# Cross-attention reassociated: query weights times memory keys and memory values times output weights formed once (one decoder layer, one core)

## The chip, the cores and the metric

One core of one Trainium2 chip runs the whole program. The metric is device time in microseconds (us) of one execution, median over the runs. The profile is that of one separately profiled execution; a profile's span runs from its first to its last instruction.

## The reference, cut to what matters

One inference step of a one-layer decoder: a prompt of 2048 tokens and 8 single-token samples, model width 1024, all float32. The layer has two windowed attentions side by side, then cross-attention into 256 memory tokens, then a ConvFFN. The change touches the cross-attention alone:

```python
def memory_kv(mem, g_mem, w_mem_kv):
    kv = rms_norm(mem, g_mem) @ w_mem_kv            # 256 memory tokens
    k, v = jnp.split(kv, 2, axis=-1)                # 4 heads of 256 each
    ...
def cross_attention(h, mk, mv, w_xq, w_xo):
    q = (h @ w_xq).reshape(N, T, X_HEADS, X_HEAD_DIM)
    s = jnp.einsum('nthd,nmhd->nhtm', q, mk) * (X_HEAD_DIM ** -0.5)
    p = jax.nn.softmax(s, axis=-1)
    o = jnp.einsum('nhtm,nmhd->nthd', p, mv).reshape(N, T, D_MODEL)
    return o @ w_xo
```

The prompt's memory keys and values are computed and are outputs too. Each of the 8 samples has memory keys and values of its own, from a cache.

## The kernel before, in words

**Stages.** First the combined input projection of the prompt, with the windowed attentions woven between its tiles; then the memory keys and values (`mem_pieces`, L1640) woven between the last attention work and the first merges; then four chunks of 512 tokens. A chunk c is `pre` (L1266: output projection `w_out`, cross-attention) and `ffn` (L1442). The 8 samples ride along as 8 more columns (512 to 519): through `w_out` and the query projection in chunk 2, through the cross-attention's output projection and the ConvFFN in chunk 3. In those steps `pieces` (L843) cuts the 520 columns into 256 and 264.

**Products.** A float32 operand is split into a high part (`hi_of`, L107, ScalarE) and the rest (`lo_of`, L118, VectorE), and each product is three matmuls: high by high, low by high, high by low (L862 to L864). Activations live in panels of 128 rows by 520 columns, two parts each, from one tag of 22 buffers (L789).

**Weights.** `WStream` (L126) loads units of 4 x 128 rows by 256 columns (512 KB) into 3 raw buffers in a fixed order (L203), splits each into one of 4 pairs of buffers, and gives them out in the same order. A unit of a 512-column chunk is used by 24 matmuls.

**Cross-attention of one chunk** (L1291 to L1439). For each head `xq` (L1306) makes queries from two units of `w_xq`, scales them by the row norm broadcast over partitions (`r_bc`, L914: one full float32 matmul) and splits them. `scores` (L1345) multiplies queries (stationary, 128 tokens) by memory keys (256 moving columns) and does the softmax; `transp` (L1375) turns the probabilities; `pvx` (L1389) multiplies by the memory values; `gemm_full` (L873) applies `w_xo` from 8 units. `load_kv` (L1294) fetches and splits keys and values per head in every chunk from DRAM, where `evac_mem` (L1623) has put them.

**Samples.** `qxs` gets the samples' queries from `xq` in chunk 2; `xs_begin` (L1179) turns them and stores them; the other `cross_steps` (L1225) run in pieces during the ConvFFN of chunk 2 and leave the result in `oxs`, which `pvx` copies into the panels in chunk 3.

**Order.** Program order gives the priority; at build the framework places each engine's instructions by that priority and a timeline of its own (L1753), so later work can be pulled into gaps, within dependences and buffers. All loads and stores but a few go through SyncE's one queue. `tick` (L821) issues one side step per weight unit, and every fourth time a copy of 1 MB of the caches.

Of the kernel before, what the change touches and what calls it, by code (L numbers as in the profile page):

```python
# [18 lines left out]
D = 1024  # L19
# [16 lines left out]
def tile_layer(ctx: ExitStack, tc: tile.TileContext, I, C, O):  # L36
# [49 lines left out]
    mk_d = [dram.tile([128, 512], F32, tag=f"mk_d{h}", name=f"mk_d{h}") for h in range(4)]  # L86
    mv_d = dram.tile([256, 1024], F32, tag="mv_d", name="mv_d")
# [38 lines left out]
    class WStream:  # L126
        RAW, SPL = 3, 4

        def __init__(self):
            self.units = []  # L130
            self.raw, self.spl = {}, {}
            self.nr = self.ns = self.pos = 0

        def add(self, w, k0, nk, c0, ncol):
            self.units.append((w, k0, nk, c0, ncol))
# [10 lines left out]
        def split_to(self, i):  # L146
            while self.ns <= min(i, len(self.units) - 1):
# [13 lines left out]
        def get(self):  # L161
            self.split_to(self.pos)
            u = self.spl.pop(self.pos)
            self.pos += 1
            return u

# [58 lines left out]
    cache_steps.append(lambda: dma(out=p_mv, in_=mv_d))  # L225
# [590 lines left out]
    qxs = sbA.tile([128, 8, NS], F32, tag="qxs", name="qxs")  # L816
    oxs = sbA.tile([128, 2, 8, NS], F32R, tag="oxs", name="oxs")
# [361 lines left out]
    def xs_begin():  # L1179
        p = [bankA("t"), bankA("t")]  # L1180
        row = panel32("qxrow")
        for k in range(8):
            nc.tensor.transpose(p[k // 4][:NS, (k % 4) * 128:(k % 4) * 128 + 128], qxs[:, k, :], ident)
        for i in range(2):
            vec.tensor_copy(out=row[:NS, 512 * i:512 * i + 512], in_=p[i][:NS])
        dma(out=qx_d, in_=row[:NS, 0:1024])

# [28 lines left out]
    def xs_fin():  # L1216
# [5 lines left out]
        hi_of(oxs[:, 0], v, "a")  # L1222
        lo_of(oxs[:, 1], v, oxs[:, 0])

    cross_steps = [xs_begin] + [xs_score(n) for n in range(NS)] + \  # L1225
# [40 lines left out]
    def pre(c, oT, begin):  # L1266
# [24 lines left out]
        q_t, kv_t, p_t = {}, {}, {}  # L1291
        R = [None]

        def load_kv(h):  # L1294
            a, b = panel("mk"), panel("mv")
            for pn, src in ((a, mk_d[h]), (b, mv_d[:, 256 * h:256 * h + 256])):
                raw = small("kv")[:, 0:512]
                if pn is a:
                    dma(out=raw, in_=src)
                else:  # L1300
                    dma(out=raw.rearrange("p (k c) -> p k c", k=2), in_=src.rearrange("(k p) c -> p k c", p=128))
                hi_of(pn[:, 0, 0:512], raw, "a")
                lo_of(pn[:, 1, 0:512], raw, pn[:, 0, 0:512])
            kv_t[h] = (a, b)

        def xq(h):  # L1306
            pn = [panel("q"), panel("q")]
            load_kv(h)

            def first():  # L1310
                if h == 1:
                    nrm.r_tok()
                return W.get()

            def second():
                if h == 1:
                    R[0] = nrm.r_bc()
                    for go in late:
                        go()
                return W.get()  # L1320

            def ev(m, pi, a, b, p):
                scaled(m, a, b, p[:, 0:b - a])

            def scaled(m, a, b, p):
                f = small("qf")
                vec.tensor_tensor(out=f[:, a:b], in0=p, in1=R[0][:, a:b], op=ALU.mult)
                if b > 512:
# [5 lines left out]
            def raw(m, pi, a, b, p):  # L1334
                if pi == 0:
                    fs[m] = small("qf")
# [420 lines left out]
```

## Time and profile before

| | |
|---|---|
| median of 3 runs | 3233.0 us (3232.56 to 3245.07) |
| profiled execution, its own time | 3230.24 us |
| its span | 3228.5 us, 58044 instructions |
| TensorE matmuls | 22290, busy 96% of the span |
| VectorE / ScalarE / GpSimd busy | 67% / 44% / 31% |
| mean granted TensorE clock | 0.984 |

The span is 1.7 us shorter than the profiled execution's own time, which is 2.8 us under the median. "Busy" of TensorE counts overlapping matmuls' records as one stretch; how fast it goes is read from the distance between starts. In the chain of waits each piece is what the end waited for at that moment.

### The profile page before, as it was taken

How to read it: one execution, taken by the hardware profiler on the slowest of the kernel's cores; microseconds unless marked ns; L12 is line 12 of the kernel's file. 1: busy time of each engine (PE TensorE's matmuls, PEld its weight loads, DVE VectorE, ACT ScalarE, POOL GpSimd, SP SyncE). 2: the span in 40 equal slices, each digit the busy share in tenths (PEclk: the TensorE clock that was granted, in tenths of full speed). 3: DMA queues.
4: the chain of work that ended last, by engine and by line, in shares of the span. 5: the costliest groups of instructions: out<-in, count | busy, mean ns of one | idle time of the engine just before them, and what ended most of it. 6: DMA issues, size and time to landing. Idle time of an engine off the chain costs nothing.

```text
span 3228.5 us, 58044 instructions
## 1 busy us (share of the span) xinstructions
PE 3100.5 (96%) x22290; PEld 2713.9 (84%) x22290; DVE 2147.1 (67%) x4299; ACT 1417.1 (44%) x2793; POOL 1013.7 (31%) x959
## 2 busy tenths in 40 slices
PE   8999989889888999999999999999999999999999
PEld 8998888788877888888887778798877778999998
DVE  7687677787886667665567766555687665554544
ACT  3555654666665444223444333444433343432322
POOL 2711613224244046342205524320554332110102
PEclk9999999998899999999999999999999999999999
DMA  6899999999897346664525555453476445223231
GB/s 211 249 253 237 270 243 230 252 242 220 191 231 230 119 152 209 204 198 162 207 97 184 169 168 183 144 196 111 159 240 235 157 151 179 73 86 96 89 95 64
DMA packets 621837, 580.14 MB, mean 180 GB/s; under 512 B 264140, under 2 KB 554104, under 8 KB 620432
## 3 DMA queue, kind: packets, MB, share of 16 engines
q1 hardware_dynamic: 616808, 572.21, 60.6%
q10 hardware_dynamic: 4608, 4.20, 0.4%
q8 instruction: 175, 2.87, 0.4%
q14 instruction: 102, 0.84, 0.1%
q0 software_dynamic: 144, 0.03, 0.0%
HBM read 457.55 MB, written 136.66 MB: 184 GB/s over the span
## 4 chain that ended last, share of the span: by engine, by line
PE 64%; DVE 7%; DMA 7%; POOL 3%; issue 3%; ACT 2%; SPq 1%; POOLq 0%; DVEq 0%; ACTq 0%
PE g L863 18%; PE g L862 18%; PE g L864 18%; DMA pT<-p 4%; PE s L1358 1%; PE g L1398 1%; PE o L585 1%; DVE wl L120 1%; DVE p L570 1%; DVE sm L556 1%; DMA kx<-in_cache_mem_k_dram 1%; PE g L672 1%; PE g L674 1%; PE g L673 1%; DMA mrg<-o_d 1%
## 5 line engine op out<-in xcount | busy, mean ns | idle before, releaser
L120 DVE TENSOR_TENSOR wl<-wr,wh 128x1024 fp32r<-128x1024 f32 (+1 forms) x406 | 535.7, 1320 | 359.8 <-ACT wh L110 358.3
L110 ACT ACTIVATE wh<-wr 128x1024 fp32r<-128x1024 f32 (+1 forms) x444 | 460.8, 1040 | 674.5 <-PE g L864 382.7
L863 PE MATMUL g<-h,wl 128*128 128x512 f32 (+2 forms) x2080 | 729.5, 351 | 0.0
L862 PE MATMUL g<-h,wh 128*128 128x512 f32 (+2 forms) x2080 | 729.5, 351 | 0.0
L864 PE MATMUL g<-h,wh 128*128 128x512 f32 (+2 forms) x2080 | 725.1, 349 | 0.0
L862 PEld LDWEIGHTS g<-h,wh 128*128 128x128 f32 x2080 | 390.7, 188 | 58.6 <-issue 1.0
L864 PEld LDWEIGHTS g<-h,wh 128*128 128x128 f32 x2080 | 391.2, 188 | 55.2 <-issue 0.5
L863 PEld LDWEIGHTS g<-h,wl 128*128 128x128 f32 x2080 | 390.8, 188 | 54.9 <-issue 1.4
L672 PE MATMUL g<-wh,xh 128*128 128x256 f32 x1152 | 340.4, 296 | 1.1 <-ACT z L383 0.7
L674 PE MATMUL g<-wh,xl 128*128 128x256 f32 x1152 | 333.1, 289 | 0.3 <-DVE xl L120 0.3
L673 PE MATMUL g<-wl,xh 128*128 128x256 f32 x1152 | 331.8, 288 | 0.0
L862 PE MATMUL g<-act,wh 128*128 128x512 f32 (+2 forms) x880 | 310.4, 353 | 8.2 <-ACT act L110 5.7
L863 PE MATMUL g<-act,wl 128*128 128x512 f32 (+2 forms) x880 | 309.4, 352 | 0.0
L864 PE MATMUL g<-act,wh 128*128 128x512 f32 (+2 forms) x880 | 308.0, 351 | 0.0
L561 ACT ACTIVATE sm<-sm,ost 128x256 f32<-128x256 f32 (+1 forms) x512 | 234.8, 460 | 155.1 <-DVE ost L559 154.4
L892 POOL TENSOR_TENSOR sq<-sq 128x512 f32<-128x512 f32 (+1 forms) x83 | 125.2, 1508 | 484.2 <-ACT sq L887 451.3
L672 PEld LDWEIGHTS g<-wh,xh 128*128 128x128 f32 x1152 | 223.5, 194 | 6.4 <-ACT z L383 0.9
L674 PEld LDWEIGHTS g<-wh,xl 128*128 128x128 f32 x1152 | 222.9, 193 | 4.0 <-DVE xl L120 1.2
L673 PEld LDWEIGHTS g<-wl,xh 128*128 128x128 f32 x1152 | 223.3, 194 | 2.1 <-issue 0.2
L862 PE MATMUL g<-oT,wh 128*128 128x512 f32 (+2 forms) x608 | 216.1, 356 | 4.5 <-ACT oT L110 4.5
L863 PE MATMUL g<-oT,wl 128*128 128x512 f32 (+2 forms) x608 | 215.9, 356 | 0.0
L864 PE MATMUL g<-oT,wh 128*128 128x512 f32 (+2 forms) x608 | 211.6, 355 | 0.0
(353 smaller groups left out, 6084.2 us busy)
## 6 DMA issues: line engine op xcount, KB each, us to landing
wr<-in_w_up_dram SPq DMA_DIRECT2D x176, 512.0 KB
wr<-in_w_down_dram SPq DMA_DIRECT2D x80, 512.0 KB
out_dram<-in_cache_a_k_dram SPq DMA_DIRECT2D x32, 1023.5 KB
out_dram<-in_cache_a_v_dram SPq DMA_DIRECT2D x32, 1023.5 KB
wr<-in_w_in_dram SPq DMA_DIRECT2D x60, 512.0 KB
v<-va_d SPq DMA_DIRECT2D x60, 384.0 KB
wr<-in_w_out_dram SPq DMA_DIRECT2D x32, 512.0 KB
wr<-in_w_xq_dram SPq DMA_DIRECT2D x32, 512.0 KB
```

The lines of the kernel that those rows point to most:

```text
L110: act(out=out, in_=in_, func=ACTF.Copy)
L120: e.tensor_tensor(out=out, in0=in_, in1=hi.bitcast(F32), op=ALU.subtract)
L556: vec.tensor_tensor_reduce(out=sm[:, x, 0:n], in0=S[e][:, u * n:(u + 1) * n], in1=m_, scale=1.0, scalar=-3e38, op0=ALU.add, op1=ALU.max, a ...
L561: act(out=sm[:, x, 0:n], in_=sm[:, x, 0:n], func=ACTF.Exp, scale=0.125, bias=nb[:, x:x + 1], accum_out=job.ost[:, 520 + 4 * i + x:521 + 4 ...
L570: vec.tensor_tensor(out=p2[:, 1], in0=sm[:, :, 0:n], in1=p2[:, 0], op=ALU.subtract)
L672: mm(p[:, 0:256], h[:, kt, :], wh[:, q, :], start=(kt == 0), stop=False)
L673: mm(p[:, 0:256], h[:, kt, :], wl[:, q, :], start=False, stop=False)
L674: mm(p[:, 0:256], l[:, kt, :], wh[:, q, :], start=False, stop=(kt == 7))
L862: mm(o, wh[:, q, c], pn[:, 0, a:b], start=st, stop=False)
L863: mm(o, wl[:, q, c], pn[:, 0, a:b], start=False, stop=False)
L864: mm(o, wh[:, q, c], pn[:, 1, a:b], start=False, stop=en)
L892: pl.tensor_tensor(out=acc[:, 0:self.ncol], in0=acc[:, 0:self.ncol], in1=sq[:, 0:self.ncol], op=ALU.add)
```

## The change

The keys of head h are folded into the query weights (`qk_d` = w_xq_h times keys transposed, 1024 x 256 per head), and the values into the output weights (`vo_d` = values times w_xo_h, 256 x 1024 per head). Both are made once between the attention and chunk 0, stored to DRAM, and streamed as weight units in every chunk. `scores` now multiplies normalised tokens (stationary) by units of `qk_d` (256 moving columns, 1024 deep instead of 256), and the turned probabilities are multiplied by `vo_d` directly; the row norm enters as the scale of the softmax. `xq`, `load_kv`, `pvx` and the query's `r_bc` go. The samples, whose keys are their own, get their query and output projections by themselves from units of `w_xq` (chunk 2) and `w_xo` (chunk 3) that only they use (`sample_rows`). The memory values are turned and stored like the keys, and written to their output from SBUF rather than copied later.

```diff
+        self.whole = set()
...
-            while self.ns <= min(i, len(self.units) - 1):
+            while self.ns <= min(i, len(self.units) - 1) and self.ns not in self.whole:
...
+    def get_whole(self):
+        self.load_to(self.pos)
...
+    for h in range(4):
+        for hf in range(2):
+            W.add(w_xq, 4 * hf, 4, 256 * h, 256, whole=True)
+        for hf in range(2):
+            W.add(w_xo, 2 * h, 2, 512 * hf, 512)
     for c in range(4):
         add_full(w_out)
-        add_full(w_xq)
-        add_full(w_xo)
+        add_full(qk_d)
+        if c == 2:
+            add_full(w_xq)
+        if c == 3:
+            add_full(w_xo)
+        for mps, khs in (((0, 1), (0,)), ((0, 1), (1,)), ((2,), (0, 1)), ((3,), (0, 1))):
+            for kh in khs:
+                for mp in mps:
+                    W.add(vo_d, 4 * kh, 4, 256 * mp, 256)
...
-    cache_steps.append(lambda: dma(out=p_mv, in_=mv_d))
...
-    cross_steps = [xs_begin] + [xs_score(n) for n in range(NS)] + \
+    cross_steps = [xs_score(n) for n in range(NS)] + \
...
         def scores(h):
+            S = [bank("s", 2) if h % 2 == 0 else bank("g", 4) for _ in range(2)]
+            for kh in range(2):
+                w = W.get()
+                for t in range(4):
+                    for q in range(4):
+                        pn = h1[4 * kh + q]
+                        for a, b in ((0, 0), (0, 1), (1, 0)):
+                            mm(S[t // 2][:, t % 2 * 256:t % 2 * 256 + 256], pn[:, a, t * 128:t * 128 + 128], w[b][:, q, :],
...
+                W.ahead(2)
+                tick()
+            if h == 0:
+                r = sbA.tile([128, 4], F32, tag="r16", name="r16", bufs=2)
+                vec.tensor_scalar(out=r, in0=nrm.r_tok()[:, 0:4], scalar1=0.0625, scalar2=None, op0=ALU.mult)
...
+        def sample_rows(scale, done):
+            row = panel32("srow")
+            for mp in range(4):
+                p = bankA("t")
+                for kh in range(2):
+                    wh, wl = W.get()
+                    for q in range(4):
+                        k = 4 * kh + q
+                        parts = [(p[:NS, 0:256], las[:, k, 0:NS], wl), (p[:40, 0:256], las[:, k, :], wh)]
+                        for o, x, w in parts if k else reversed(parts):
+                            mm(o, x, w[:, q, :], start=(k == 0 and w is wh), stop=(k == 7 and w is wh))
+                    W.ahead(2)
...
+        for h in range(4):
+            scores(h)
+            if h:
+                transp(h - 1)
...
+        if s_in:
+            sample_rows(nrm.r[:NS, 4:5], keep_q)
+        if s_out:
+            sample_rows(None, add_xo)
+        gemm_two(pT, ev_xo, lambda: transp(3))
+        gemm_full(pT, pieces(False), ev_xo, range(2, 4))
...
+        dma(out=(p_mk if j < 4 else p_mv)[tok, cols], in_=z)
+        pt = bankA("t")
+        for dt in range(2):
+            nc.tensor.transpose(pt[:, dt * 128:dt * 128 + 128], z[:, dt * 128:dt * 128 + 128], ident)
+        zt = small("mz")[:, 0:256]
+        act(out=zt, in_=pt[:, 0:256], func=ACTF.Copy)
+        dma(out=mkv_d[j].rearrange("p (k t) -> p k t", k=2)[:, :, tok], in_=zt.rearrange("p (k t) -> p k t", k=2))
...
+    def mem_q(h, hf, mk):
+        w = W.get_whole()
+        T = []
+        for dt in range(2):
+            pt = bankA("t")
+            for q in range(4):
+                nc.tensor.transpose(pt[:, q * 128:(q + 1) * 128], w[:, q, dt * 128:dt * 128 + 128], ident)
+            pn = panel("wT")
+            hi_of(pn[:, 0, 0:512], pt, "a")
+            lo_of(pn[:, 1, 0:512], pt, pn[:, 0, 0:512])
+            T.append(pn)
...
+        for fp in range(2):
+            p = bank("g", 4)
+            for f in range(2):
+                fb = 2 * fp + f
+                for dt in range(2):
+                    for a, b in THREE:
+                        mm(p[:, f * 256:f * 256 + 256], T[dt][:, a, fb * 128:fb * 128 + 128],
+                           mk[:, b, dt * 256:dt * 256 + 256], start=(f == 0 and dt == 0 and a + b == 0),
...
+            store_w(p, "a", qk_d[r0:r0 + 256, 256 * h:256 * h + 256].rearrange("(f p) c -> p f c", p=128))
+    def mem_o(h, hf, mv):
+        w = W.get()
+        W.ahead(1)
+        for kb in range(2):
+            p = bank("g", 4)
+            for dt in range(2):
+                for a, b in THREE:
+                    mm(p, mv[:, a, dt * 256 + kb * 128:dt * 256 + kb * 128 + 128], w[b][:, dt, :],
...
+            store_w(p, "v", vo_d[(2 * h + kb) * 128:(2 * h + kb + 1) * 128, 512 * hf:512 * hf + 512])
+    for h in range(4):
+        mk = mem_panel(h)
+        for hf in range(2):
+            mem_q(h, hf, mk)
+        mv = mem_panel(4 + h)
+        for hf in range(2):
+            mem_o(h, hf, mv)
     oT = []
     for go in heads_T(0, oT):
         go()
```

In what is left out, `gemm_two` takes the first four `vo_d` units depth half by depth half, with 24 matmuls of 512 columns each; `mem_panel` loads one `mkv_d` panel (256 KB) and splits it; `store_w` evacuates a bank and stores 256 KB.

## Rows read from the trace of the kernel before

**Rows 1.** The page's first part: busy time (share of the span) and instructions.

```profile
PE 3100.5 (96%) x22290; PEld 2713.9 (84%) x22290; DVE 2147.1 (67%) x4299; ACT 1417.1 (44%) x2793; POOL 1013.7 (31%) x959
```

**Rows 2.** Waits of TensorE, longest in total first: us, times, longest.

```profile
PE o L585 <- DMA pT<-p: 43.1, 34, 2.8
...
PE g L862 <- ACT act L110: 5.7, 2, 4.7
```

**Rows 3.** Busy time by stretch of the span, with granted clock, DMA share, GB/s.

```profile
core 0: us, PE busy (x) PEld busy (x) DVE busy (x) ACT busy (x) POOL busy (x), PEclk, DMA share, GB/s
860.00:980.00 120.00, 100.05 (x1323) 90.24 (x1321) 101.63 (x309) 82.14 (x232) 58.38 (x40) 0.94 1.00 233
980.00:1000.00 20.00, 11.41 (x177) 10.41 (x176) 14.62 (x19) 9.81 (x19) 7.46 (x5) 0.97 1.06 287
1000.00:1040.00 40.00, 40.00 (x181) 32.46 (x180) 24.01 (x38) 17.74 (x29) 12.91 (x10) 0.97 0.65 219
1048.00:1165.00 117.00, 116.42 (x569) 96.64 (x568) 68.71 (x117) 51.77 (x97) 11.35 (x8) 1.00 0.37 124
...
2710.00:2830.00 120.00, 120.00 (x774) 108.77 (x773) 71.19 (x128) 54.34 (x100) 18.02 (x25) 1.00 0.28 90
```

**Rows 4.** The chain of waits in chunk 0's cross-attention: start, us, what.

```profile
1067.40 0.86 PE t L922 x2
...
1107.79 2.78 PE g L1398 x12
1110.57 0.87 PE t L1381 x8
1111.44 2.83 PE s L1358 x24
```

**Rows 5.** TensorE's timeline in chunk 3: start, us, instruction; 6 and 12 starts lie between these.

```profile
2900.01 0.29 PE L862 MATMUL g<-h,wh 128*128 128x264 f32 x1
...
2900.75 0.28 PE L862 MATMUL g<-h,wh 128*128 128x256 f32 x1
...
2902.16 0.28 PE L862 MATMUL g<-h,wh 128*128 128x264 f32 x1
```

**Rows 6.** Line 1358 (scores): weight loads, ns min/median/max, first and last start.

```profile
L1358 PEld LDWEIGHTS s<-mk,q x384: 187/188/192, 1074.6 to 2776.2; 128*128 128x128 f32 x192
```

**Rows 7.** TensorE's timeline, sample columns of the input projection (40 and 8 rows).

```profile
664.48 0.29 PE L771 MATMUL g<-wh,la 128*40 128x256 f32 x1
664.60 0.28 PE L771 MATMUL g<-wl,lb 128*8 128x256 f32 x1
664.72 0.28 PE L771 MATMUL g<-wh,la 128*40 128x256 f32 x1
```

**Rows 8.** Waits of SyncE's queue: us in total, times, longest.

```profile
SPq L141 <- DVE wl L120: 1365.3, 295, 24.7
```

**Rows 9.** ScalarE and VectorE by form, 1040 to 1170 us: busy, mean ns, idle before.

```profile
L110 ACT ACTIVATE wh<-wr 128x1024 fp32r<-128x1024 f32 x18 | 19.1, 1060 | 34.6 <-PE g L864 17.2 <-issue 13.2 <-ACT sq L887 3.4
L110 ACT ACTIVATE pT<-t 128x512 fp32r<-128x512 f32 x8 | 4.3, 596 | 6.7 <-PE t L1381 6.6
...
L120 DVE TENSOR_TENSOR wl<-wr,wh 128x1024 fp32r<-128x1024 f32 x19 | 23.6, 1241 | 22.5 <-ACT wh L110 22.2
L1363 DVE TENSOR_REDUCE st<-s 128x2 f32<-128x512 f32 x8 | 5.5, 686 | 2.1 <-PE s L1358 2.1
L120 DVE TENSOR_TENSOR pT<-t,pT 128x512 fp32r<-128x512 f32 x8 | 5.3, 685 | 4.7 <-ACT pT L110 4.7
L1370 DVE TENSOR_SCALAR pe<-pe,st 128x256 f32<-128x256 f32 x16 | 4.9, 348 | 0.2
```

**Rows 10.** The chain of waits: weight loads, end of the issue to landing.

```profile
978.05 4.39 DMA wr<-in_w_out_dram
...
992.91 4.85 DMA wr<-in_w_out_dram
```

**Rows 11.** Line 1636: the store of turned keys, ns of an issue on SyncE's queue.

```profile
L1636 SPq DMA_DIRECT2D mk_d<-mz x8: 529/536/553, 885.4 to 943.8; - x8
```

**Rows 12.** TensorE's timeline after a wait; 12 starts lie from the second to the third.

```profile
2062.05 0.80 PE L862 MATMUL g<-act,wh 128*128 128x512 f32 x1 [4.71 <-ACT act L110]
...
2065.31 0.63 PE L863 MATMUL g<-act,wl 128*128 128x512 f32 x1
...
2070.43 0.56 PE L863 MATMUL g<-act,wl 128*128 128x512 f32 x1
```

More of the change, by code (lines that the diff above doesn't have):

```diff
@@ L165, in get @@
             return u
+        def get_whole(self):
+            assert self.pos == self.ns and self.pos in self.whole
+            self.load_to(self.pos)
+            w, k0, nk, c0, ncol = self.units[self.pos]
+            r = self.raw.pop(self.pos)
+            self.pos += 1
+            self.ns += 1
+            return r[:, 0:nk * ncol].rearrange("p (k c) -> p k c", k=nk)
         def ahead(self, n):
@@ L1288, in pre @@
         del oT[:]
[L1291 to L1328, printed above, removed]
-                    pl.tensor_copy(out=qxs[:, 2 * h + m, :], in_=f[:, 512:NC])
-                    b = 512
-                hi_of(pn[m][:, 0, a:b], f[:, a:b], "a")
-                lo_of(pn[m][:, 1, a:b], f[:, a:b], pn[m][:, 0, a:b])
-            def raw(m, pi, a, b, p):
-                if pi == 0:
-                    fs[m] = small("qf")
-                act(out=fs[m][:, a:b], in_=p[:, 0:b - a], func=ACTF.Copy)
-                late.append(lambda: scaled(m, a, b, fs[m][:, a:b]))
-            fs = {}
-            gemm_b([(first, [0, 1, 2, 3]), (second, [4, 5, 6, 7])], h1, pieces(s_in), raw if s_in and h == 0 else ev,
-                   late if h == 0 and not s_in else None)
-            q_t[h] = pn
@@ L1345, in scores @@
[L1345 to L1360 removed]
+        p_t = {}
@@ L1426, in pre, with keep_q, add_xo @@
+        def keep_q(row):
+            dma(out=qx_d, in_=row[:NS, 0:1024])
+        def add_xo(row):
+            pt = bankA("t")
+            for k in range(8):
+                nc.tensor.transpose(pt[:, k * NS:(k + 1) * NS], row[:NS, k * 128:(k + 1) * 128], ident[:NS, :NS])
+            vec.tensor_tensor(out=xs1, in0=pt[:, 0:64].rearrange("p (k n) -> p k n", k=8), in1=xs1, op=ALU.add)
         h2 = [None] * 8
@@ L1678, in conv_out, with mem_panel, store_w @@
         return go
+    def mem_panel(j):
+        pn = panel("mkv")
+        raw = small("kv")[:, 0:512]
+        dma(out=raw, in_=mkv_d[j])
+        hi_of(pn[:, 0, 0:512], raw, "a")
+        lo_of(pn[:, 1, 0:512], raw, pn[:, 0, 0:512])
+        return pn
+    def store_w(p, eng, out):
+        z = small("az")[:, 0:512]
+        hi_of(z, p, eng)
+        dma(out=out, in_=z if len(out.shape) == 2 else z.rearrange("p (f c) -> p f c", f=2))
+    THREE = ((0, 0), (0, 1), (1, 0))
+    def mem_q(h, hf, mk):
+        w = W.get_whole()
+        T = []
+        for dt in range(2):
+            pt = bankA("t")
+            for q in range(4):
+                nc.tensor.transpose(pt[:, q * 128:(q + 1) * 128], w[:, q, dt * 128:dt * 128 + 128], ident)
+            pn = panel("wT")
+            hi_of(pn[:, 0, 0:512], pt, "a")
+            lo_of(pn[:, 1, 0:512], pt, pn[:, 0, 0:512])
+            T.append(pn)
+        W.load_to(W.pos + 1)
+        W.ahead(1)
[7 more added lines that the diff above has]
+                           mk[:, b, dt * 256:dt * 256 + 256], start=(f == 0 and dt == 0 and a + b == 0),
+                           stop=(dt == 1 and a == 1), skip_group_check=True)
+            r0 = (4 * hf + 2 * fp) * 128
+            store_w(p, "a", qk_d[r0:r0 + 256, 256 * h:256 * h + 256].rearrange("(f p) c -> p f c", p=128))
+    def mem_o(h, hf, mv):
+        w = W.get()
+        W.ahead(1)
+        for kb in range(2):
[3 more added lines that the diff above has]
+                    mm(p, mv[:, a, dt * 256 + kb * 128:dt * 256 + kb * 128 + 128], w[b][:, dt, :],
+                       start=(dt == 0 and a + b == 0), stop=(dt == 1 and a == 1))
+            store_w(p, "v", vo_d[(2 * h + kb) * 128:(2 * h + kb + 1) * 128, 512 * hf:512 * hf + 512])
[6 more added lines that the diff above has]
+            mem_o(h, hf, mv)
     oT = []
```

146 lines of the change are left out of this document (57 added, 89 removed).

## The prediction

> **What bounds the kernel now.** I read the page's first part first: TensorE's matmuls are busy 96% of the span, and no other engine is over VectorE's 67% [rows 1]. Next, what TensorE waits for: most is one item, the transposing loads of the attention stage, which ends before 1000 us, and the longest waits among the chunks are single ones of a few us [rows 2]. The busy time by stretch then shows two regimes [rows 3]. From 1000 us on TensorE has no gap worth naming; the cross-attention of chunk 0 (1048 to 1165) is busy 116.42 of 117 us and that of chunk 3 120 of 120. So in the chunks a matmul less is its time less, and nothing hides a matmul more. From 860 to 980 us it is the other way round: TensorE is busy 100 of 120 us, and the DMA share is 1.00 at 233 GB/s. Right behind, 980 to 1000, TensorE works 11.41 of 20 us at a share of 1.06. The change takes matmuls out of the first regime and puts new ones, with many transfers, between the two.
>
> **Prices of a matmul.** Durations overlap, so I take distances. The chain has 12 matmuls of 512 columns in 2.78 us, 0.232 each; 24 of 256 columns in 2.83 us, 0.118 each; 8 transposes in 0.87 us, 0.109 each [rows 4]. A 256-column matmul costs half of a 512-column one, which the whole idea needs. The 264-column ones cost 0.123 (6 in 0.74 us) and the 256-column ones beside them 0.1175 (12 in 1.41 us) [rows 5], so 512 columns plus samples cost 0.241 instead of 0.232.
>
> **What goes, per chunk.** Queries: 8 units x 24 = 192 matmuls of 512 columns. Values: 4 heads x 12 = 48. Together 240 x 0.232 = 55.7 us. Scores were 4 x 24 = 96 matmuls of 256 columns and become 4 heads x 2 units x 48 = 384: 288 more x 0.118 = 34.0 us. The output product stays at 192 of 512, the 32 transposes stay. Net 21.7 us a chunk, **87 us** in four. The queries of chunk 2 and the output product of chunk 3 lose their cut into 256 and 264: 2 x 192 x 0.009 = 3.5 us. The row norm's broadcast matmul of 0.86 us [rows 4] goes four times: 3.4 us. Sum of what goes: **94 us**. The evacuations of queries and values and the 32 key and value loads go too, off the path: I cost them at nothing, since TensorE covers VectorE (busy 69 of 117 us) and ScalarE (52) there [rows 3]. The next softmax is not late: each head's two banks have the next head's 96 x 0.118 = 11.3 us as cover, against two reductions of 0.69 and four scalings of 0.35 on VectorE [rows 9].
>
> **What comes, 1: the folding.** Per head 48 matmuls of 256 columns and 16 transposes for the query side, 24 of 512 columns for the value side. Four heads: 192 x 0.118 + 64 x 0.109 + 96 x 0.232 = 22.7 + 7.0 + 22.3 = **52 us** of TensorE. Nothing is there to hide it: chunk 0's `w_out` units stand behind the 16 new units in the weight order. Transfers: 16 units of 512 KB, 8 panels of 256 KB, and 32 stores of 256 KB, 18.9 MB. The trace has no such stage, so I bound its rate by two rows: 219 GB/s at a share of 0.65 is 337 GB/s with all engines busy (1000 to 1040), and 233 GB/s at 1.00 is what the attention stage reached [rows 3]. That is 56 us or 81 us. VectorE per head: two panels, four weight panels and four stores, ten times about 0.69, plus two splits of 1.24, is 9.4 us of 13; ScalarE less [rows 9]. I take the first rate, since the units and panels move in pieces like the weight loads of the chunks and not like transposing loads: 56 us, and about 5 us for the first load to land before anything runs (4.39 and 4.85 us under load [rows 10]): **62 us**, between 52 (TensorE alone) and 86. SyncE issues 56 transfers at about 0.54 us [rows 11], 30 us in all; but a store that waits for its evacuation holds the weight loads behind it in the same queue, and TensorE waits for those. This is why I do not go below 62. The 32 store and load round trips end long before chunk 0 reads its first folded unit, behind 45 us of `w_out`.
>
> **What comes, 2: the sample rows.** In chunks 2 and 3, 8 units with 8 matmuls each of 256 columns: 64 x 0.118 = 7.5 us, 15 us in both; the same form elsewhere comes every 0.12 us [rows 7]. But a unit then lasts TensorE 0.95 us instead of 5.6, and needs 1.06 us of ScalarE and 1.24 us of VectorE to split [rows 9]. The weight stream now runs full: SyncE waits 1365 us in all for a raw buffer to be split [rows 8], so on arrival three units are split ahead and three loaded. Units 3 to 8 (the sixth of these is the first `vo_d` unit) still need 6 x 1.24 = 7.4 us of VectorE, beside the last softmax (3.5 us from the rows above), two probability panels (1.4) and four row evacuations (about 1.5 together): 13.8 us. By the loads it is similar: unit 6 can be issued only when unit 3 is split, 2.3 us on, lands 4.4 later at the worst, and takes 2.3 to split. From 13.8 I take off 1.7 us of transposes that fill the gap: **12 us** each, 24 in both. Lower bound 7.5 each, upper 15.5: a wait of 4.71 us was followed by matmuls at 0.427 us distance (12 in 5.12 us), half the clock (1.2 of 2.4 GHz), until 2070.4 [rows 12], about 3.5 us more.
>
> **What comes, 3: the tail of the attention stage.** Values are now turned like keys: 16 transposes (1.7 us), 8 more stores at 0.54 us on SyncE [rows 11], 1 MB more where DMA is at 1.00 [rows 3], 4.5 us. These lie beside each other: **4 us**, from 0 (into the 8.6 us that TensorE idles from 980 to 1000) to 10. What else waits in that queue is the attention's own transposing loads. The cache copies lose one of 1 MB and the four chunks lose 2 ticks each: nothing, since some 557 us of TensorE a chunk (3228.5 less 1000, by four) cover them.
>
> **Sum.** 62 + 24 + 4 - 94 = -4 us. The sum is made against the profiled execution (3230.24 us); the median is 2.8 us above it, and I put the change on the median: 3233 - 4 = **3229 us**. With TensorE's matmuls alone it would be 52 + 15 + 2 - 94 = -25: most of that gain is lost to starving stretches.
>
> **The rivals.**
>
> *Faster: the starving doesn't happen.* The scheduler pulls the sample matmuls and the folding's loads so that both run at TensorE's pace: -25 us, 3208; where the folding also starts inside the 8.6 idle us before 1000, 3200. For it: buffers are full on arrival, and DMA from 1048 on is at 0.37 [rows 3]. Against it: the unit order is fixed, and 18.9 MB in 52 us is 363 GB/s, more than any row shows.
>
> *Slower: the folding is transfer-bound at the attention's rate.* The first stores and loads queue behind the attention's last transfers, and loads behind stores that wait for their evacuation. At 233 GB/s it takes 81 + 5 = 86 us, the sample rows 15.5 each at half clock, the tail 6: 86 + 31 + 6 - 94 = +29, 3262 us. It decides once the folding takes over 82 us with the rest as forecast. For it: 860 to 1000 us. Against: few small packets are left by then. The Trainium skill, "TensorE: Matmul & The Clock Gate", section "HAM oscillation — how this bites in real kernels", describes short bursts of matmuls between DMA waits that fall back to the slow clock each time. Rows 12 agree for a wait of 4.71 us; whether it happens in the folding no row shows.
>
> *Much slower: the 256-column matmuls are bound by their weight loads.* Each load's record lasts 188 ns [rows 6], longer than 118. If loads didn't overlap in long runs, 1536 score matmuls and 192 of the folding would cost 0.070 more each: 121 us, 3350. Against it: the 24 in 2.83 us have a load each. The Trainium skill, "Perfetto Trace Analysis", section "Identifying the Most-Contended Engine", takes the busy share of weight loads as a measure of how near TensorE is to its limit, and would speak against a change that doubles the loads per column. In chunk 3 loads are busy 109 of 120 us at an undisturbed pace [rows 3], so here the distance decides, not that share.
>
> **How the numbers follow.** About no change 0.42 (its own range 3217 to 3249, that is 0.5% either way, about what a measurement of this kernel can tell from no change); faster rival 0.34; slower rival 0.21; much slower 0.03. The range goes from the faster rival with the idle filled, 3200, to the slower rival, 3262; left out are the much slower one and the outer parts of the two others, under 2 in 10. Faster 0.34, same 0.42, slower 0.24.
>
> **What would show it.** Right: 20 to 22 us less from the start of scores to the end of the output product in chunks 0 and 1; 384 score matmuls a chunk at 0.118; a stretch of about 62 us between the last attention matmul and `w_out`, with a DMA share near 0.9 and TensorE at some 85%; gaps of 4 to 5 us in all behind the scores of chunks 2 and 3, released by weight splits. Wrong: a folding stretch of 52 or of over 80 us; score matmuls at 0.19; sample rows with no gap; or a chunk that is not 20 us shorter, by a softmax that TensorE waits for.

## The result and the profile after

The changed kernel takes **3269.7 us** (median of 4 runs, 3264.74 to 3274.73), the kernel before 3232.8 beside it: ratio 1.0106, 95% interval 1.0086 to 1.0125. That is 37 us slower, where I forecast 4 us faster and a range that ended at 3262. The profiled execution took 3269.64 us (span 3267.9). The budget below goes by the two traces.

Busy time on the page of the changed kernel, to be held against [rows 1]:

```profile
PE 3103.2 (95%) x22584; PEld 2733.0 (84%) x22584; DVE 2123.1 (65%) x4209; ACT 1415.6 (43%) x2760; POOL 1017.9 (31%) x952
```

TensorE is as busy as before over a span that is 39 us longer. Two time stamps cut the span where it matters: the first `w_out` matmul of chunk 0, in TensorE's timeline of the kernel before, and then of the changed one:

```profile
999.44 0.80 PE L862 MATMUL g<-oT,wh 128*128 128x512 f32 x1 [4.52 <-ACT oT L110]
```

```profile
1116.51 0.47 PE L887 MATMUL g<-oT,wh 128*128 128x512 f32 x1
```

From there to the end the kernel before needs 3228.5 - 999.4 = 2229.1 us, the changed one 3267.9 - 1116.5 = 2151.4. The chunks give back **77.7 us**, against 70 forecast (94 less 24 for the sample rows). The loss is ahead of that stamp, 117.1 us. TensorE's timeline of the changed kernel where the folding starts:

```profile
1006.42 0.44 PE L1628 MATMUL t<-ident,mz 128*128 128x128 f32 x2 [3.28 <-ACT mz L1622]
1006.69 1.75 PE L1695 MATMUL t<-ident,wr 128*128 128x128 f32 x8
1010.98 1.22 PE L1708 MATMUL g<-mkv,wT 128*128 128x256 f32 x4 [2.54 <-ACT wT L111]
```

L1628 turns the last memory panel, L1695 turns units of `w_xq`, L1708 multiplies them by keys, L1721 multiplies values by `w_xo`. The folding begins at 1006.7, 7.3 us after the stamp of the kernel before (the tail, forecast 4), and lasts to 1116.5: **109.8 us**, forecast 62. 7.3 + 109.8 - 77.7 = 39.4, the difference of the spans.

The stretches of the folding, and chunk 0's cross-attention behind it, in busy time (columns as in [rows 3]):

```profile
1006.00:1020.00 14.00, 8.95 (x52) 7.68 (x52) 6.30 (x16) 5.44 (x12) 0.00 (x0) 0.76 0.72 224
1020.00:1040.00 20.00, 11.83 (x46) 9.62 (x46) 6.94 (x11) 5.97 (x12) 7.26 (x6) 0.78 0.75 242
...
1060.00:1080.00 20.00, 11.77 (x73) 10.79 (x71) 6.22 (x9) 6.03 (x10) 0.00 (x0) 0.83 0.52 157
...
1125.00:1222.00 97.00, 97.00 (x630) 87.91 (x629) 54.65 (x85) 40.57 (x75) 12.14 (x8) 1.00 0.44 147
```

In the folding's six stretches nothing is full: TensorE works 9 to 15 of 14 to 20 us at a mean granted clock of 0.74 to 0.83, the DMA share is 0.47 to 0.75, VectorE and ScalarE are busy 30 to 49%. Chunk 0 has no gap. Such a picture, every engine half idle, fits a chain in which each link waits for the one before. TensorE's waits from 990 to 1130 us name the last link:

```profile
PE g L1708 <- ACT wT L111: 19.4, 5, 5.6
PE g L1721 <- ACT mkv L111: 15.6, 4, 4.5
```

Both name ScalarE, which is busy only some 6 of 20 us, so one has to ask what it waits for. One period, in SyncE's timeline, ScalarE's and TensorE's:

```profile
1059.96 2.18 SPq L1685 DMA_DIRECT2D vo_d<-az  x3
1062.19 1.30 SPq L1677 DMA_DIRECT2D kv<-mkv_d  x1
1063.55 0.42 SPq L1685 DMA_DIRECT2D vo_d<-az  x1
```

```profile
1055.56 1.06 ACT L111 ACTIVATE wh<-wr 128x1024 fp32r<-128x1024 f32 x1 [1.02 <-DMA wr<-in_w_xo_dram]
1066.44 0.63 ACT L111 ACTIVATE mkv<-kv 128x512 fp32r<-128x512 f32 x1 [9.82 <-DMA kv<-mkv_d]
1066.97 1.07 ACT L111 ACTIVATE wT<-t 128x512 fp32r<-128x512 f32 x2
```

```profile
1049.60 0.60 PE L1695 MATMUL t<-ident,wr 128*128 128x128 f32 x4
...
1060.67 0.85 PE L1721 MATMUL g<-wh,mkv 128*128 128x512 f32 x3
...
1067.60 2.50 PE L1708 MATMUL g<-mkv,wT 128*128 128x256 f32 x10 [5.61 <-ACT wT L111]
```

The load of the next keys (L1677) stands in SyncE's queue behind stores of the head before (L1685), which wait for the evacuations of matmuls that ran until 1061. So it leaves at 1062.2, lands at 1066.4, ScalarE takes its high part after 9.82 idle us, and only then, in its order, copies transposes that TensorE had made at 1050 (L1695, 1049.60). TensorE resumes at 1067.6. The next load leaves when the next stores do. SyncE's waits from 1000 to 1120 us show the same hold in sum:

```profile
SPq L1685 <- ACT az L111: 38.0, 10, 9.1
SPq L1685 <- DVE az L115: 16.8, 12, 9.0
```

For 55 of the 110 us SyncE stands at a store, and what comes behind it in the queue, loads too, stands with it. The second loss is the clock. TensorE's timeline after another of these waits:

```profile
1054.59 0.52 PE L1721 MATMUL g<-wh,mkv 128*128 128x512 f32 x1 [4.39 <-ACT mkv L111]
1054.93 0.61 PE L1721 MATMUL g<-wl,mkv 128*128 128x512 f32 x1
1055.34 0.63 PE L1721 MATMUL g<-wh,mkv 128*128 128x512 f32 x1
...
1058.58 0.39 PE L1721 MATMUL g<-wl,mkv 128*128 128x512 f32 x1
1058.81 0.86 PE L1721 MATMUL g<-wh,mkv 128*128 128x512 f32 x3
```

The matmuls come at 0.41 us distance first, the 1.2 GHz level (granted clock 0.57 from 1054.59 to 1058.58), and at 0.23 from 1058.6 on, the 2.4 GHz level (1.00 from there to 1062.0). The folding has ten waits, 35.7 us together. Its 109.8 us are thus 52 of matmuls at full clock, 35.7 of waits, 1.7 for 16 transposes of chunk 0 that lie between them (L1265), and some 20 that are left for the slow stretches behind the waits. The Trainium skill, "TensorE: Matmul & The Clock Gate", section "HAM oscillation — how this bites in real kernels", describes this pattern of short bursts that each start cold; the trace agrees, with a granted clock of 0.50 to 0.67 over the first 1 to 4 us behind each of the nine waits of 1.6 us or more.

The scores of chunk 0 by their line, first and last start at the end of each row:

```profile
L1319 PE MATMUL s<-wh,h x128: 277/279/364, 1162.9 to 1198.5; 128*128 128x256 f32 x128
L1319 PE MATMUL g<-wh,h x128: 277/279/364, 1175.0 to 1210.7; 128*128 128x256 f32 x128
```

384 matmuls (with 128 of the low parts), 16 transposes and 8 matmuls of two columns take 47.8 us; less 24 x 0.109 for the small ones, that is 0.118 each, as in [rows 4].

The samples' rows starve for about as long as forecast. TensorE's starts behind a wait, and the first output matmul, in the rows of chunk 2, then of chunk 3:

```profile
2261.98 0.31 PE L1368 MATMUL t<-wh,las 128*40 128x256 f32 x1 [2.19 <-DVE pT L121]
2271.29 0.28 PE L1368 MATMUL t<-wl,las 128*8 128x256 f32 x1 [1.04 <-DVE wl L121]
2272.71 0.73 PE L1412 MATMUL g<-pT,wh 128*128 128x512 f32 x2
2273.97 0.50 PE L1413 MATMUL g<-pT,wl 128*128 128x512 f32 x1 [0.53 <-DVE wl L121]
...
2806.86 0.31 PE L1368 MATMUL t<-wh,las 128*40 128x256 f32 x1 [2.18 <-DVE pT L121]
...
2818.18 1.22 PE L1412 MATMUL g<-pT,wh 128*128 128x512 f32 x2 [3.23 <-ACT wh L111]
```

From the first sample matmul to the first output matmul it is 10.7 us in chunk 2, where the output then waits once more, and 11.3 in chunk 3, where some sample matmuls still lie behind it. Ahead of each row there is a wait of 2.2 us, for the split of the probabilities (`pT`); the later ones of half a us and more name the split of weights, as forecast.

### The profile page after: what moved, and what is told of

The parts are those of the page before. It is cut to its first block, busy times and chain, and to the rows that moved or that the text cites. A ratio compares the mean times of both kernels' runs of the same rounds, so it can differ in the third digit from the quotient of the medians.

```text
span 3267.9 us, 58603 instructions
## 1 busy us (share of the span) xinstructions
PE 3103.2 (95%) x22584; PEld 2733.0 (84%) x22584; DVE 2123.1 (65%) x4209; ACT 1415.6 (43%) x2760; POOL 1017.9 (31%) x952
## 5 line engine op out<-in xcount | busy, mean ns | idle before, releaser
L121 DVE TENSOR_TENSOR wl<-wr,wh 128x1024 fp32r<-128x1024 f32 (+1 forms) x430 | 569.1, 1324 | 393.4 <-ACT wh L111 392.3
L111 ACT ACTIVATE wh<-wr 128x1024 fp32r<-128x1024 f32 x468 | 485.7, 1041 | 777.3 <-PE g L889 343.7
L888 PE MATMUL g<-h,wl 128*128 128x512 f32 (+2 forms) x1760 | 616.5, 350 | 1.4 <-DVE wl L121 1.4
L887 PE MATMUL g<-h,wh 128*128 128x512 f32 (+2 forms) x1760 | 617.2, 351 | 0.0
L889 PE MATMUL g<-h,wh 128*128 128x512 f32 (+2 forms) x1760 | 613.7, 349 | 0.0
L887 PEld LDWEIGHTS g<-h,wh 128*128 128x128 f32 x1760 | 330.8, 188 | 50.2 <-issue 0.7
L888 PEld LDWEIGHTS g<-h,wl 128*128 128x128 f32 x1760 | 330.8, 188 | 48.2 <-DVE wl L121 1.8
L889 PEld LDWEIGHTS g<-h,wh 128*128 128x128 f32 x1760 | 330.9, 188 | 47.0
L121 POOL TENSOR_TENSOR wl<-wr,wh 128x1024 fp32r<-128x1024 f32 x38 | 96.5, 2540 | 346.4 <-ACT wh L111 308.6
L610 PEld LDWEIGHTS <-pT 128*128 128x128 f16 x4240 | 145.7, 101 | 66.9 <-DMA pT<-p 57.1
L595 DVE TENSOR_TENSOR p<-sm,p 128x1024 f16<-128x1024 f32 (+1 forms) x128 | 151.5, 1184 | 62.3 <-ACT p L594 61.9
```

What stands on the lines that cost most here:

```text
L111: act(out=out, in_=in_, func=ACTF.Copy)
L121: e.tensor_tensor(out=out, in0=in_, in1=hi.bitcast(F32), op=ALU.subtract)
L595: vec.tensor_tensor(out=p2[:, 1], in0=sm[:, :, 0:n], in1=p2[:, 0], op=ALU.subtract)
L610: mm(o, p_[:, hf, x, :], v[:, g, :], start=(x == 0 and hf == 0 and n_ == 0), stop=(hf == nh - 1 and n_ == 4), skip_group_check=True)
L887: mm(o, wh[:, q, c], pn[:, 0, a:b], start=st, stop=False)
L888: mm(o, wl[:, q, c], pn[:, 0, a:b], start=False, stop=False)
```

## The experiments

**Theory:** the folding is a serial chain, panel load behind stores, buffers, ScalarE's order, and its length is that of the chain's waits. **Rivals:** it is bound by its transfers, or by TensorE at a low clock, or the loss is in the chunks. To compare the profiled executions I use the time from the start of the last transpose of a memory panel (L1628 above, the second of the two: 1006.6 in the changed kernel) to the first `w_out` matmul: it leaves out the attention stage, whose end lay anywhere from 997 to 1008 us in these traces.

| kernel | median us | ratio to before, 95% | last transpose to `w_out`, us | `w_out` to the end, us |
|---|---|---|---|---|
| the change | 3269.69 | 1.0106 (1.0086 to 1.0125) | 109.9 | 2151.4 |
| folding left out | 3167.65 | 0.9792 (0.976 to 0.9824) | 2.6 | 2158.5 |
| sample rows left out | 3238.94 | 1.0002 (0.9989 to 1.0014) | 110.4 | 2125.1 |
| panels early | 3254.71 | 1.0062 (1.0041 to 1.0083) | 96.6 | 2151.6 |
| stores on ScalarE's queue | 3257.7 | 1.0069 (1.0047 to 1.009) | 98.5 | 2153.8 |
| both of these | 3254.57 | 1.0064 (1.0039 to 1.0088) | 98.0 | 2156.1 |
| early, panel parts on GpSimd | 3241.08 | 1.0021 (1.0006 to 1.0036) | 83.5 | 2153.2 |
| early, panels in wide buffers | 3241.78 | 1.0017 (1.0 to 1.0033) | 83.5 | 2157.8 |
| units deep | 3241.59 | 1.002 (1.0008 to 1.0032) | 84.3 | 2153.0 |
| units deep, stores on ScalarE's | 3234.66 | 0.9999 (0.9987 to 1.0012) | 79.2 | 2151.1 |
| mixed | 3241.18 | 1.0017 (1.0004 to 1.0029) | 84.4 | 2152.2 |
| mixed, rows spread | 3225.55 | 0.9969 (0.9957 to 0.9981) | 84.9 | 2139.0 |
| the same, panel parts on GpSimd | 3220.09 | 0.9944 (0.9926 to 0.9961) | 76.9 | 2138.7 |

The last column falls only where the samples' rows were touched; elsewhere it lies between 2151.1 and 2158.5, and every other gain is ahead of `w_out`. The kernel before, measured anew beside each group of runs, had medians from 3232.8 to 3236.9, so a difference between rows of different groups is good to a few us only.

### The folding left out

```diff
-            W.add(w_xq, 4 * hf, 4, 256 * h, 256, whole=True)
...
-        add_full(qk_d)
+        add_full(w_xq)
...
-                    W.add(vo_d, 4 * kh, 4, 256 * mp, 256)
+                    W.add(w_xo, 4 * kh, 4, 256 * mp, 256)
...
-    for h in range(4):
-        mk = mem_panel(h)
-        for hf in range(2):
-            mem_q(h, hf, mk)
...
```

> The folding is left out and the chunks stream the plain query and output weights in its place, so scores and output are others; all else stays. It measures the folding's price by itself. Chain theory: the folding's 110 us are all on the path: 3270 - 110 = 3160. If part of the folding hides other work (the first turning of heads, loads for chunk 0, the tail of the attention), it is less by that part; the forecast's 62 us would give 3208. The chunks alone should stand 75 to 80 us under those of the kernel before.

3167.65 us (two runs), 102 below the changed kernel: nearly all of the 110 is on the path. The folding costs 102 us, and without its price the rest of the change would be worth 2% of the kernel. The chunks stand 70.6 us under those of the kernel before (2229.1 - 2158.5), not 75 to 80, but they are far from slower: the rival that the loss is in the chunks falls.

### The sample rows left out

```diff
-        if c == 2:
-            add_full(w_xq)
-        if c == 3:
-            add_full(w_xo)
...
-            sample_rows(nrm.r[:NS, 4:5], keep_q)
-        if s_out:
-            sample_rows(None, add_xo)
...
```

A copy and a fill stand in for the query rows, which the samples' attention reads.

> The changed kernel with the samples' query and output projections of chunks 2 and 3 left out, with their sixteen weight units. My prediction took 12 us for each row, 24 in all: about 3246 against 3269.7. Rival (the rows hide other waits that come back without them): 3258 or more; rival (they cost their transfers and splits too, later in the chunks): 3235 or less.

3238.94, 31 us below the changed kernel, between the forecast and the last rival. The column from `w_out` to the end is cleaner: 2151.4 - 2125.1 = **26.3 us** for both rows, against 24 forecast; the profiled executions differ by 32.9, and the rest of that is the attention's end, 7 us earlier in this one. It also gives the chunks without the rows: 2229.1 - 2125.1 = 104.0 us, where I had 94. Of the missing 10, the waits for `act` of 5.7 us in the kernel before [rows 2] and the slow stretch behind them [rows 12], about 3.5, have no counterpart here; that they are the reason is argued, not shown.

### Panels early

The key and value panels are loaded and split two half-heads ahead.

```diff
+    turns = [0, 4, 1, 5, 2, 6, 3, 7]
+    pans = {j: mem_panel(j) for j in turns[:2]}
+    for i, j in enumerate(turns):
+        if i + 2 < 8:
+            pans[turns[i + 2]] = mem_panel(turns[i + 2])
...
-            mem_q(h, hf, mk)
+            (mem_q if j < 4 else mem_o)(j % 4, hf, pans[j])
```

> Each key or value panel of the folding is loaded two half-heads ahead of its use, nothing else differs. Chain theory: in the changed kernel the folding lasts 110 us (1006.7 to 1116.5) because each panel load stands in SyncE's queue behind stores that wait for their evacuation, and ScalarE, in order, holds the split of the turned weights behind the panel; eight landings are paid one after the other, 33 us of waits of 2.5 to 5.6 us on TensorE, and the clock falls to half in each. Then loads issued early free all of it: folding 60 to 70 us, time 3220 to 3230. Rival A, the weight units are what is late (three raw buffers, loads behind stores): the panels are there early and TensorE waits for the units instead: folding 95 us or more, time above 3254. Rival B, transfer-bound: folding stays at 81 us or more at a DMA share of 1.0.

3254.71, 15 us less, and the stretch is 96.6 us where the theory said 60 to 70: a miss for it. The time is that of rival A, but TensorE does not wait for the units. The waits for value panels are gone, those for the turned weights have grown. Waits of TensorE from 1000 to 1130 us, then ScalarE's timeline in one of them:

```profile
PE g L1708 <- ACT wT L111: 31.9, 4, 11.1
```

```profile
1057.45 1.06 ACT L111 ACTIVATE wh<-wr 128x1024 fp32r<-128x1024 f32 x1 [5.24 <-DMA wr<-in_w_xo_dram]
1060.06 0.63 ACT L111 ACTIVATE mkv<-kv 128x512 fp32r<-128x512 f32 x1 [1.56 <-DMA kv<-mkv_d]
1064.39 0.63 ACT L111 ACTIVATE mkv<-kv 128x512 fp32r<-128x512 f32 x1 [3.70 <-DMA kv<-mkv_d]
1064.93 1.06 ACT L111 ACTIVATE wT<-t 128x512 fp32r<-128x512 f32 x2
```

ScalarE works in order, and the copy that TensorE needs (`wT`) stands behind a panel that nobody needs yet. Here the early load only moved the wait, since the early item held the late one.

### Stores on ScalarE's queue, and both

```diff
-        dma(out=out, in_=z if len(out.shape) == 2 else z.rearrange("p (f c) -> p f c", f=2))
+        nc.scalar.dma_start(out=out, in_=z if len(out.shape) == 2 else z.rearrange("p (f c) -> p f c", f=2))
```

> The 32 stores of folded weights are issued from ScalarE's queue instead of SyncE's; the panel loads keep their place in the program. Chain theory with the stores as the holder: panel loads and unit loads no longer wait for evacuations, so the waits of 4 to 6 us per panel shrink: folding 65 to 80 us, time 3225 to 3240. If it is not the stores but the place of the load in the program and ScalarE's order that count: folding stays above 95 us, time above 3254, and ScalarE's issues may add to it.

> Panels loaded ahead and stores on ScalarE's queue together. Chain theory: little beyond the better of the two alone, folding 55 to 65 us, time 3215 to 3228, since TensorE alone needs 52. Rival A (weight units late behind stores): both are needed, so this one is faster than either alone by 15 us or more.

3257.7 for the stores alone, 12 us less: loads that no longer queue behind stores. The stretch stays at 98.5 us, so the stores are one holder and not the only one. Both together take 3254.57, the same as the early panels alone, and TensorE waits 33.5 us for `wT`. That is neither the 55 to 65 us of the theory nor the gain of 15 over either that rival A needs. The two edits don't add: by the wait that is left, another holder of the chain ends last.

### Early, with the panels' parts on GpSimd

```diff
-        hi_of(pn[:, 0, 0:512], raw, "a")
-        lo_of(pn[:, 1, 0:512], raw, pn[:, 0, 0:512])
+        hi_of(pn[:, 0, 0:512], raw, "p")
+        lo_of(pn[:, 1, 0:512], raw, pn[:, 0, 0:512], "p")
```

> As the version with panels loaded two half-heads ahead (3254.7), and the two parts of each panel are made on GpSimd, which is idle there, instead of ScalarE and VectorE. There a panel that is not needed yet held ScalarE, which works in order: four waits of TensorE of 4.7 to 11.1 us, 32 us in all, named the turned weights behind it. If ScalarE's order is what made the early load useless: those waits go, folding 60 to 75 us, time 3220 to 3235. If the load itself is late (its buffer or its place in SyncE's queue): TensorE waits as long, for the panel by name, time 3248 to 3262.

3241.08, 13.6 below the early panels alone. TensorE's waits, 1000 to 1130 us:

```profile
PE g L1708 <- issue: 6.9, 2, 3.7
PE g L1708 <- ACT wT L111: 4.4, 2, 3.3
```

31.9 us for `wT` has become 4.4; for 6.9 more the profile shows no cause. The stretch, 83.5 us, is above the 60 to 75 expected, so ScalarE's order is one holder and not the last. (The edit relieves VectorE of the low parts too; that it was ScalarE's order goes by the lines of the run before.)

### Early, with the panels in wide buffers

The stores (`az`) and the raw panels (`kv`) share seven small buffers, so a panel's load can wait for a store to land. Here the panels get others.

```diff
-        raw = small("kv")[:, 0:512]
+        raw = panel32("kv")[:, 0:512]
```

> As the version with panels loaded two half-heads ahead, and the raw panel goes into one of the 22 wide buffers instead of one of the 7 small ones that the stores of folded weights also use. If the small buffers, each held until its store has landed, are what holds the loads back: panel loads leave 10 us earlier, folding 65 to 80 us, time 3222 to 3240. If only ScalarE's order or the weight units hold: no change from 3254.7 within 6 us.

3241.78, 12.9 below the early panels alone, with a stretch of 83.5 us instead of the 65 to 80 expected; the wait for `wT` falls from 31.9 in four to 20.4 in two:

```profile
PE g L1708 <- ACT wT L111: 20.4, 2, 12.4
```

The buffers are another holder. GpSimd and wide buffers together were not run on the early panels.

### Units deep, and with the stores on ScalarE's queue

The folding's weight units leave the weight stream and are loaded five ahead into wide buffers; panels three ahead, in wide buffers too.

```diff
+    turns = [0, 4, 1, 5, 2, 6, 3, 7]
+    pans = {j: mem_panel(j) for j in turns[:3]}
+    units = {i: unit(i) for i in range(5)}
+    for i in range(16):
...
+        if i + 5 < 16:
+            units[i + 5] = unit(i + 5)
+        (mem_q if j < 4 else mem_o)(j % 4, i % 2, pans[j], units.pop(i))
```

> The folding's 16 weight units no longer go through the weight stream with its 3 raw buffers but are loaded five ahead into wide buffers, and panels three ahead, also into wide buffers; the weight stream loads the first output-projection units meanwhile. Stores stay on SyncE. If the folding is a chain of late loads and not bound by transfers or TensorE: folding 58 to 70 us, between TensorE's 52 and the transfers' 56 plus one landing, time 3215 to 3230. If stores in the same queue still hold the loads: 80 us or more, 3238 or more.

> As the version with units five ahead, and the stores go out from ScalarE's queue. If stores on SyncE still hold loads: 10 us or more below it, and down to 3210 to 3220. If the loads are far enough ahead: the same within 5 us, or some us slower by ScalarE's issues.

3241.59 and 3234.66. The first is what was expected if stores in the same queue still hold the loads; the second is 7 us below it, between the 10 of that theory and the 5 of its rival. With the stores out of SyncE's queue, this is the folding at TensorE's pace (columns as in [rows 3]), behind one long wait:

```profile
1010.00:1020.00 10.00, 1.97 (x8) 1.57 (x8) 5.27 (x14) 2.09 (x4) 4.56 (x4) 0.50 1.06 377
1030.00:1082.00 52.00, 51.10 (x334) 45.89 (x334) 32.24 (x51) 27.27 (x51) 0.00 (x0) 1.00 0.73 242
```

```profile
PE t L1701 <- DMA wu<-in_w_xq_dram: 14.3, 1, 14.3
PE g L1712 <- ACT wT L111: 5.6, 1, 5.6
```

334 matmuls in 52 us at full clock, at a DMA share of 0.73. So neither the transfers nor the clock bounds the folding behind its start: the clock stays up once the waits are gone, and both rivals fall there. What is left is the start: SyncE issues the first unit's load only at 1010.65, 8 us after the last transpose, and the first units land in a stretch at a share of 1.06. There the transfers may well be the limit. That the wide buffers come free only when the attention ends was my reading; no line here shows it.

### Mixed

Head 0's four units come through the weight stream again, which is filled during the attention, and the first two panels through small buffers.

```diff
+    for hf in range(2):
+        W.add(w_xq, 4 * hf, 4, 0, 256, whole=True)
+    for hf in range(2):
+        W.add(w_xo, 0, 2, 512 * hf, 512)
...
-        raw = panel32("kv")[:, 0:512]
+        raw = (small if j in (0, 4) else panel32)("kv")[:, 0:512]
```

> The run with deep buffers and the stores on ScalarE's queue (3234.66) still waits 14.29 + 5.63 us at the folding's start, because its buffers come free only when the attention ends and its weight units stand in SyncE's queue behind other loads. Here head 0's four units come through the weight stream's own buffers again, which are filled during the attention, and the first key and value panels through the small buffers; everything else is as in that run. Theory (the start is lateness of those first loads): the first folding matmul comes near 1008 instead of 1024.5 and w_out's first near 1066 to 1070, so about 3218 to 3222. Rival (the transfers of the remaining twelve units, 6.3 MB with the panels, cannot land in time however they are ordered, since the DMA share is 1.06 there): the wait moves to head 1's units, and the time stays at 3230 to 3236.

A miss: 3241.18, 6.5 us more than the run it was to beat (0.0018 by the ratios, some 6 us). Neither theory names what happened. Head 0's units are there, TensorE turns them at 1002.5, and then waits 16.0 us for the copies. The lines of the next run below show why.

### Rows spread

```diff
-        if s_in:
-            sample_rows(nrm.r[:NS, 4:5], keep_q)
-        if s_out:
-            sample_rows(None, add_xo)
...
+            if s_in:
+                sample_rows(nrm.r[:NS, 4:5], keep_q, h)
+            if s_out:
+                sample_rows(None, add_xo, h)
```

The units of `w_xq` and `w_xo` stand behind each head's two of `qk_d` in the weight order.

> As the mixed run, and the samples' query and output projections, which consume eight weight units in one row in chunks 2 and 3, are spread over the four heads' scores (two units behind each head's 96 matmuls). Theory (in the row the weight split cannot keep up: some 11 to 12 us each, of which the matmuls alone are about 4): 6 to 8 us less in each of two chunks, so 12 to 16 us under the mixed run, about 3204 to 3210, clear below the kernel before. Rival (the price is the matmuls' own, or the wait moves to the softmax behind the first scores): within 4 us of the mixed run.

3225.55: 15.6 below the mixed run, inside the 12 to 16 expected, and faster than the kernel before (the absolute time I had expected rested on the mixed run's miss). From `w_out` to the end it is 13.2 us shorter than the mixed run. The two rows now cost 2139.0 - 2125.1 = 13.9 us, which is about their 128 matmuls (15.1 at 0.118). The long wait at the start is still there. TensorE had turned the first unit by 998.8; its wait, and ScalarE's timeline from there:

```profile
PE g L1719 <- ACT wT L111: 16.7, 1, 16.7
```

```profile
1000.33 0.63 ACT L111 ACTIVATE mkv<-kv 128x512 fp32r<-128x512 f32 x1 [2.38 <-DMA kv<-mkv_d]
1003.08 0.63 ACT L111 ACTIVATE mkv<-kv 128x512 fp32r<-128x512 f32 x1 [2.12 <-DMA kv<-mkv_d]
1005.32 1.06 ACT L111 ACTIVATE wh<-wr 128x1024 fp32r<-128x1024 f32 x1 [1.61 <-DMA wr<-in_w_xo_dram]
1006.81 1.06 ACT L111 ACTIVATE wh<-wr 128x1024 fp32r<-128x1024 f32 x1 [0.43 <-DMA wr<-in_w_out_dram]
1008.90 0.63 ACT L111 ACTIVATE mkv<-kv 128x512 fp32r<-128x512 f32 x1 [1.03 <-DMA kv<-mkv_d]
...
1014.33 0.63 ACT L111 ACTIVATE mkv<-kv 128x512 fp32r<-128x512 f32 x1 [1.11 <-DMA kv<-mkv_d]
1014.87 1.07 ACT L111 ACTIVATE wT<-t 128x512 fp32r<-128x512 f32 x2
```

Each line waits a little for its own load, and `wT`, which needs none, is last.

### Rows spread, with the panels' parts on GpSimd

The edit is that of the earlier run on GpSimd.

> The spread run still waits 16.71 us in one piece at the folding's start (998.8 to 1015.50), for ScalarE's copies of transposes that were done at 998.8: in ScalarE's order they stand behind four panels' high parts, each waiting for its load, and three weight splits. Here all eight panels' high and low parts are made on GpSimd, as in the earlier run that did this. Theory (ScalarE's order is what holds it): the wait falls to that of the splits alone, 5 to 8 us, so 8 to 11 us less, about 3214 to 3218. Rival (GpSimd, which merges chunk 0's heads from 1012 to 1019 for 7 us and is slower per element, becomes the holder: a wait for its panel parts of about the same length, later the merge): 3223 to 3230.

3220.09, the fastest of the kernels that do the whole work (0.9944 of the kernel before). It lies between the theory's 3214 to 3218 and the rival's 3223 to 3230. Over the spread run it gains 5.5 us by medians; the two intervals overlap a little. The stretch from the last transpose to `w_out` is 8.0 us shorter in the trace, but only 1.9 of that is the wait itself, which is 14.8 us, not 5 to 8; the other 6 lie behind it. In these two executions `w_out` even starts 2.4 us later, since the attention ended 10 us later. So the gain is there, and the theory of the wait is not borne out. The wait, and ScalarE's timeline, which shows the next in line:

```profile
PE g L1719 <- ACT wT L111: 14.8, 1, 14.8
```

```profile
1015.46 1.06 ACT L111 ACTIVATE wh<-wr 128x1024 fp32r<-128x1024 f32 x1 [7.13 <-DMA wr<-in_w_xo_dram]
...
1022.16 1.06 ACT L111 ACTIVATE wh<-wr 128x1024 fp32r<-128x1024 f32 x1 [0.47 <-DMA wr<-in_w_out_dram]
1023.13 1.07 ACT L111 ACTIVATE wT<-t 128x512 fp32r<-128x512 f32 x2
```

The panels are gone from ScalarE, and a weight split that waits 7.13 us for its load has their place. Whether the start could be shortened by ScalarE's order alone, or whether the loads of that stretch are late in any order, was not tried further and stays open.

## Why the prediction was wrong

- **The step that failed is "What comes, 1: the folding", 62 us.** It is 109.8 us in the trace and 102 by leaving it out. The working took the largest of TensorE (52), the transfers (56 and 5 for the first landing) and VectorE (9.4 of 13 a head), as if they ran beside each other. They did not, as the period above and the gains of the later runs show: panel load, split, matmul, evacuation, store and the next panel's load followed one another. I had written that "a store that waits for its evacuation holds the weight loads behind it in the same queue" and used it only as a reason not to go lower; that sentence was the mechanism, and it had no price. A price was at hand in the rows: eight panel loads of 4.4 to 4.9 us each, as weight loads took [rows 10], are 35 to 39 us if nothing lies beside them; the ten waits measured 35.7. That the two sums meet is partly luck, since the waits are ten, of 0.6 to 5.6 us, and not eight of one length.
- **The upper bound of 86 was no bound.** It came from a transfer rate, and the actual stretch ran at 149 to 242 GB/s with the share under 0.8, so the transfers were not full. The slower rival had the right side and the right place, and named "loads behind stores that wait for their evacuation", but it priced the rate of the transfers in place of their order.
- **The clock.** I had charged a slow stretch to the sample rows at worst [rows 12], none to the folding. It came there after each long wait, and made about 20 of the 110 us.
- **What goes, 94 us:** 104.0 without the rows, the missing 10 being argued above and not shown. The parts hold: the score matmuls keep their distance, and the rival that their weight loads would bind them is refuted: at 0.070 us more each the 104 us would be gone.
- **The sample rows, 24 us:** 26.3, and the weight splits do hold TensorE there as described, beside a wait of 2.2 us for the probabilities; spread out, the rows cost 13.9 and those waits are gone. One term of the 12 us a row was misread: the softmax is 2 x 0.69 + 4 x 0.35 = 2.8 us by the rows it points to, not 3.5.
- **The tail, 4 us:** 7.3, within its bounds of 0 to 10. But the attention's end moves by 10 us between traces of kernels whose attention code is the same, so one trace could not have settled it.
- **The faster rival** ("the starving doesn't happen", 3208) was not far off what can be had: by other buffers and queues the folding came to TensorE's pace, save its start, and with the rows spread and the panels' parts on GpSimd the kernel took 3220, still 12 us above it.

## What to carry to other kernels

A new stage that loads, computes, stores and loads again through one queue may be priced by its chain, as here, and not by its busiest resource: write down one period link by link, and count every load that stands behind a store and every copy that stands behind a load. Cutting one link can only move the wait to the next: here one edit alone gave 12 to 15 us of the 58 that lie between the folding's 110 us and TensorE's 52, and it took deep buffers of its own, with the stores out of the loads' queue, for the folding to run at TensorE's pace behind its start. Units that a short piece of work consumes quickly were better spread behind long pieces than put in a row.

## What was not expected of the hardware

- A single stretch moved 377 GB/s at a share of 1.06 (1010 to 1020 us in the run with deep units and the stores on ScalarE's queue), where I had held 363 GB/s to be "more than any row shows". The Trainium skill, "Perfetto Trace Analysis", section "Roofline", gives 358 GB/s as a core's share when both cores of a pair are active and says that one core alone can draw more; this run, with one core active, agrees.
- TensorE was back at the 1.2 GHz level behind waits of 4 to 6 us also when it had reached 2.4 GHz just before: granted clock 0.57 from 1054.59 to 1058.58, 1.00 to 1062.0, then a wait of 5.61 us, and 0.50 from 1067.60 to 1071.50. In this stage the slow level was paid again behind each long wait.
